# A rotary-embedding kernel: DMA runs of 64 KB instead of 32 KB, with three resident tiles

## The chip, the cores and the metric

The kernel runs on one core of a Trainium2 chip. The metric is device time in microseconds (us), the median of several executions. The profile's span, from the first to the last instruction, is some 2 us shorter than that time. Every execution has a state: slow when it took over 1.5% more than the fastest of the same kernel, else fast, and unknown for a single run. Medians are over all executions. All TensorE clocks read 1.000, in the slow executions too; the kernel does not use TensorE.

The names used below: SBUF and PSUM are the two on-chip memories in which the kernel allocates its tiles, each tile in 128 rows called partitions; VectorE and GpSimd are the engines that compute here; SyncE and ScalarE only issue DMAs. A DMA is one transfer that the program issues; it is put into the queue of the engine that issued it, and 16 DMA engines carry it out in packets. A 64 KB run is a stretch of 64 KB that is contiguous on both sides of a transfer; otherwise a run is an execution or an experiment.

## The reference

```python
def reference(x, cos, sin):          # x (16, 512, 16, 64), cos and sin (512, 32), float32
    half_dim = dim // 2              # dim = 64
    x1, x2 = x[..., :half_dim], x[..., half_dim:]
    # cos and sin broadcast over batch and heads
    first  = x1[..., :16] * cos[..., :16] - x1[..., 16:] * sin[..., :16]
    second = x1[..., :16] * sin[..., :16] + x1[..., 16:] * cos[..., :16]
    return concatenate([first, second, x2], axis=-1)
```

The input x is 33.55 MB and the output is as large. Half of every head passes through unchanged, but the kernel moves it through SBUF with the rest, because whole rows are contiguous in memory.

## The kernel before

The flat array is cut into tiles of 128 partitions; a partition holds K consecutive sequence positions, each of H x D = 1024 numbers (4 KB). With K = 8 a partition's run is 32 KB, a tile is 4 MB, and there are eight tiles.

```python
    K = 8
    T = B * S // (P * K)          # 8 tiles
    # ...
    x_pool = ctx.enter_context(tc.tile_pool(name="xp", bufs=5))
    ab_pool = ctx.enter_context(tc.tile_pool(name="abp", bufs=1))
    # ... cos and sin are loaded on the ACT queue and copied into `table`
    KC = 4
    for t in range(T):
        x_t = x_pool.tile([P, K, H, D], fp32)
        nc.sync.dma_start(out=x_t.rearrange("p k h d -> p (k h d)"), in_=xf[t])
        for k0 in range(0, K, KC):
            x1 = x_t[:, k0 : k0 + KC, :, 0:HF]
            # c and s: the table, broadcast over the heads
            nc.vector.tensor_mul(out=a_t[:], in0=x1, in1=c)
            nc.vector.tensor_mul(out=b_t[:], in0=x1, in1=s)
            nc.vector.tensor_sub(out=x1[:, :, :, 0:Q], in0=a_t[:, :, :, 0:Q], in1=b_t[:, :, :, Q:HF])
            nc.vector.tensor_add(out=x1[:, :, :, Q:HF], in0=a_t[:, :, :, Q:HF], in1=b_t[:, :, :, 0:Q])
        nc.scalar.dma_start(out=of[t], in_=x_t.rearrange("p k h d -> p (k h d)"))
```

All loads of x are issued by SyncE (queue 1), all stores and the small cos/sin loads by ScalarE (queue 10). Both queues feed the same 16 DMA engines: in the packet records never more than 16 of these packets run at once, and loads and stores take turns in the same 16 sequences. One data packet is one partition's run (1024 packets of 32 KB in each queue, for eight DMAs of 128 partitions), so a 128-partition DMA is eight packets on each engine.

## Time and profile before

| | before |
|---|---|
| time, median | 162.38 us |
| span | 160.4 us |
| bytes moved, mean rate | 67.25 MB, 419 GB/s |
| VectorE busy | 110.8 us (69%) |
| a 32 KB packet, load or store (packet records) | 1213 ns median |

From the profile page of the kernel before: the span, the busy time of the compute engines, the DMA engines' busy tenths in 40 equal slices of the span, the packets, and, for each of the two data queues, packets, MB and the time of its packets as a share of 16 engines' span.

```profile
span 160.4 us, 155 instructions
DVE 110.8 (69%) x68; POOL 0.2 (0%) x4
...
DMA  7999999999999999999999999999999999999993
...
DMA packets 2465, 67.25 MB, mean 419 GB/s; under 512 B 288, under 2 KB 416, under 8 KB 416
...
q1 hardware_dynamic: 1152, 33.55, 49.3%
q10 hardware_dynamic: 1312, 33.69, 48.7%
```

The two queue shares add to 98.0%. 98.0% of 160.4 us is 157.2 us of packets for each engine: the DMA engines are the bound, and there is next to no time without a packet. A 32 KB packet in 1213 ns is 27.0 GB/s for one engine, or 432 GB/s for 16.

The groups of VectorE work of the same page (line, engine, operation, output and inputs with shapes, count | busy us, mean ns of one | idle before it and what ended most of it):

```profile
L65 DVE TENSOR_TENSOR a_t<-x_t,table 128x2048 f32<-128x2048 f32 x16 | 36.7, 2292 | 13.6 <-DMA x_t<-in_x_dram 13.2
L66 DVE TENSOR_TENSOR b_t<-x_t,table 128x2048 f32<-128x2048 f32 x16 | 36.5, 2284 | 0.0
L67 DVE TENSOR_TENSOR x_t<-a_t,b_t 128x1024 f32<-128x1024 f32 x16 | 19.6, 1226 | 0.6
L70 DVE TENSOR_TENSOR x_t<-a_t,b_t 128x1024 f32<-128x1024 f32 x16 | 19.5, 1218 | 0.0
```

VectorE waits for data, 13.2 us in all, and has 49.6 us to spare. The same bound is seen by stage in the windows of the kernel before (stretch in us, its length, VectorE busy, GpSimd busy, clock, mean busy share of the DMA engines, GB/s):

```profile
36.00:100.00 64.00, 61.66 (x37) 0.00 (x0) 1.00 1.01 434
130.00:158.00 28.00, 12.01 (x8) 0.00 (x0) 1.00 1.00 432
```

While loads and stores run together the engines move 434 GB/s, and at the end, with stores alone, 432.

### The profile page before, as it was taken

The numbers are of one execution on the slowest core, as the hardware profiler recorded it, in microseconds if no ns is written. First come the engines' busy times: TensorE is split into PE (matmuls) and PEld (weight loads), VectorE is DVE, ScalarE is ACT, GpSimd is POOL, SyncE is SP. The second block draws the span as 40 slices with busy tenths as digits, with TensorE's granted clock in tenths as the row PEclk, the third lists the DMA queues.
The fourth block names the chain that finished last, engine by engine and source line by source line (L and its number), as shares of the span: only waits on it lengthen the run. The fifth ranks groups of instructions, "written<-read, shape, count | busy, mean of one in ns | idle before, by whom it ended". The sixth has DMA issues, their size and how long they took to land.

```text
span 160.4 us, 155 instructions
## 1 busy us (share of the span) xinstructions
DVE 110.8 (69%) x68; POOL 0.2 (0%) x4
## 2 busy tenths in 40 slices
DVE  0001599999999999999998799609995099940000
POOL 0000000000000000000000000000000000000000
DMA  7999999999999999999999999999999999999993
GB/s 253 408 400 408 392 417 490 400 408 498 400 400 474 433 392 457 457 392 449 466 392 417 490 400 408 498 400 400 476 425 400 466 441 400 449 457 400 417 482 147
DMA packets 2465, 67.25 MB, mean 419 GB/s; under 512 B 288, under 2 KB 416, under 8 KB 416
## 3 DMA queue, kind: packets, MB, share of 16 engines
q1 hardware_dynamic: 1152, 33.55, 49.3%
q10 hardware_dynamic: 1312, 33.69, 48.7%
q14 instruction: 1, 0.01, 0.0%
HBM read 33.69 MB, written 33.55 MB: 419 GB/s over the span
## 4 chain that ended last, share of the span: by engine, by line
DMA 53%; DVE 30%; issue 4%; DVEq 1%; ACTq 0%; SPq 0%
DMA x_t<-in_x_dram 21%; DMA out_dram<-x_t 21%; DVE b_t L66 11%; DMA stage<-in_sin_dram 10%; DVE a_t L65 10%; DVE x_t L70 5%; DVE x_t L67 4%; DVEq L99 1%; ACTq L41 0%; DVE table L48 0%; SPq L58 0%; DVEq L65 0%
## 5 line engine op out<-in xcount | busy, mean ns | idle before, releaser
L65 DVE TENSOR_TENSOR a_t<-x_t,table 128x2048 f32<-128x2048 f32 x16 | 36.7, 2292 | 13.6 <-DMA x_t<-in_x_dram 13.2
L66 DVE TENSOR_TENSOR b_t<-x_t,table 128x2048 f32<-128x2048 f32 x16 | 36.5, 2284 | 0.0
L67 DVE TENSOR_TENSOR x_t<-a_t,b_t 128x1024 f32<-128x1024 f32 x16 | 19.6, 1226 | 0.6
L70 DVE TENSOR_TENSOR x_t<-a_t,b_t 128x1024 f32<-128x1024 f32 x16 | 19.5, 1218 | 0.0
L48 DVE COPY table<-stage 64x256 f32<-64x256 f32 x4 | 1.1, 287 | 17.1 <-DMA stage<-in_cos_dram 12.2
L88 POOL MEMSET const-bfloat16-1.0<- 128x1 bf16 x1 | 0.1, 102 | 0.0
L88 POOL MEMSET const-uint8-127<- 128x1 uint8 x1 | 0.1, 102 | 0.0
L88 POOL MEMSET const-float32-0.0<- 128x1 f32 x1 | 0.1, 99 | 0.2 <-issue 0.2
L88 POOL MEMSET const-float32-1.0<- 128x1 f32 x1 | 0.1, 99 | 0.0
## 6 DMA issues: line engine op xcount, KB each, us to landing
x_t<-in_x_dram SPq DMA_DIRECT2D x8, 4096.0 KB, 33.9
out_dram<-x_t ACTq DMA_DIRECT2D x8, 4096.0 KB, 31.3
stage<-in_cos_dram ACTq DMA_DIRECT2D x1, 64.0 KB, 11.4
stage<-in_sin_dram ACTq DMA_DIRECT2D x1, 64.0 KB, 16.3
```

The costliest lines, as they stand in the source:

```text
L48: nc.vector.tensor_copy(out=table[r * PB : (r + 1) * PB, t], in_=stage[:, t, :, 0:Q].unsqueeze(2).to_broadcast((PB, K, 2, Q)),)
L65: nc.vector.tensor_mul(out=a_t[:], in0=x1, in1=c)
L66: nc.vector.tensor_mul(out=b_t[:], in0=x1, in1=s)
L67: nc.vector.tensor_sub(out=x1[:, :, :, 0:Q], in0=a_t[:, :, :, 0:Q], in1=b_t[:, :, :, Q:HF])
L70: nc.vector.tensor_add(out=x1[:, :, :, Q:HF], in0=a_t[:, :, :, Q:HF], in1=b_t[:, :, :, 0:Q])
L88: nc = _bacc.Bacc("TRN2", target_bir_lowering=False, num_devices=1)
L99: with _tile.TileContext(nc) as tc:
```

## The change

The intent: runs twice as long (64 KB, K = 16, four tiles of 8 MB), so fewer packets; an earlier start, because the first tile's load comes in parts of 4, 4 and 8 positions; a fine-grained end, because the last tile is loaded and stored in halves; and the scratch in PSUM with an in-place multiply, so that no scratch lies in SBUF beside the three 8 MB tiles. With three tile buffers and four tiles, the last tile's load has to wait until the first tile's store has landed.

```diff
-    K = 8
+    K = 16
...
-    x_pool = ctx.enter_context(tc.tile_pool(name="xp", bufs=5))
-    ab_pool = ctx.enter_context(tc.tile_pool(name="abp", bufs=1))
+    x_pool = ctx.enter_context(tc.tile_pool(name="xp", bufs=3))
+    b_pool = ctx.enter_context(tc.tile_pool(name="bp", bufs=2, space=bass.MemoryType.PSUM))
...                                  (table: two larger copies on VectorE, two on GpSimd)
+    loads = [[4, 4, 8]] + [[16]] * (T - 2) + [[8, 8]]
+    stores = [[16]] * (T - 1) + [[8, 8]]
...
+        for n in loads[t]:
+            nc.sync.dma_start(
+                out=x_f[:, k0 * R : (k0 + n) * R], in_=xf[t, :, k0 * R : (k0 + n) * R]
+            )
+            k0 += n
...
-            nc.vector.tensor_mul(out=a_t[:], in0=x1, in1=c)
             nc.vector.tensor_mul(out=b_t[:], in0=x1, in1=s)
+            nc.vector.tensor_mul(out=x1, in0=x1, in1=c)
...                                  (the subtraction and the addition read x1 in place of a_t)
-        nc.scalar.dma_start(out=of[t], in_=x_t.rearrange("p k h d -> p (k h d)"))
+            for lo, hi in ends:
+                if hi == k0 + KC:
+                    nc.scalar.dma_start(
+                        out=of[t, :, lo * R : hi * R], in_=x_f[:, lo * R : hi * R]
+                    )
```

More of the change, by code (lines that the diff above doesn't have):

```diff
@@ L29 @@
     REP = P // PB
+    R = H * D
     xf = x.rearrange("b s h d -> (b s h d)").rearrange("(t p f) -> t p f", t=T, p=P)
@@ L46 @@
     for r in range(REP):
-        for t in range(2):
-            nc.vector.tensor_copy(
-                out=table[r * PB : (r + 1) * PB, t],
-                in_=stage[:, t, :, 0:Q].unsqueeze(2).to_broadcast((PB, K, 2, Q)),
-            )
+        eng = nc.vector if r % 2 == 0 else nc.gpsimd
+        eng.tensor_copy(
+            out=table[r * PB : (r + 1) * PB].rearrange("p t k c j -> p (t k) c j"),
+            in_=stage.rearrange("p t k j -> p (t k) j")[:, :, 0:Q]
+            .unsqueeze(2)
+            .to_broadcast((PB, 2 * K, 2, Q)),
+        )
     C = table[:, 0].rearrange("p k c j -> p k (c j)")
@@ L55 @@
     KC = 4
+    loads = [[4, 4, 8]] + [[16]] * (T - 2) + [[8, 8]]
+    stores = [[16]] * (T - 1) + [[8, 8]]
     for t in range(T):
         x_t = x_pool.tile([P, K, H, D], fp32)
-        nc.sync.dma_start(out=x_t.rearrange("p k h d -> p (k h d)"), in_=xf[t])
+        x_f = x_t.rearrange("p k h d -> p (k h d)")
+        k0 = 0
+        for n in loads[t]:
[3 more added lines that the diff above has]
+            k0 += n
+        ends, k0 = [], 0
+        for n in stores[t]:
+            ends.append((k0, k0 + n))
+            k0 += n
         for k0 in range(0, K, KC):
@@ L62 @@
             s = Sn[:, k0 : k0 + KC].unsqueeze(2).to_broadcast((P, KC, H, HF))
-            a_t = ab_pool.tile([P, KC, H, HF], fp32)
-            b_t = ab_pool.tile([P, KC, H, HF], fp32)
-            nc.vector.tensor_mul(out=a_t[:], in0=x1, in1=c)
+            b_t = b_pool.tile([P, KC, H, HF], fp32)
             nc.vector.tensor_mul(out=b_t[:], in0=x1, in1=s)
+            nc.vector.tensor_mul(out=x1, in0=x1, in1=c)
             nc.vector.tensor_sub(
-                out=x1[:, :, :, 0:Q], in0=a_t[:, :, :, 0:Q], in1=b_t[:, :, :, Q:HF]
+                out=x1[:, :, :, 0:Q], in0=x1[:, :, :, 0:Q], in1=b_t[:, :, :, Q:HF]
             )
             nc.vector.tensor_add(
-                out=x1[:, :, :, Q:HF], in0=a_t[:, :, :, Q:HF], in1=b_t[:, :, :, 0:Q]
+                out=x1[:, :, :, Q:HF], in0=x1[:, :, :, Q:HF], in1=b_t[:, :, :, 0:Q]
             )
-        nc.scalar.dma_start(out=of[t], in_=x_t.rearrange("p k h d -> p (k h d)"))
+            for lo, hi in ends:
+                if hi == k0 + KC:
+                    nc.scalar.dma_start(
+                        out=of[t, :, lo * R : hi * R], in_=x_f[:, lo * R : hi * R]
+                    )
 _INS = ['x', 'cos', 'sin']
```

## The prediction

> **What bounds the kernel now.** The DMA engines. The page shows 67.25 MB at 419 GB/s, the two data queues busy 49.3% + 48.7%, and DMA at 9 tenths in all slices but the first and last. VectorE is busy 110.8 of 160.4 us and waits 13.2 us for loads (waits). In the packet records a 32 KB packet takes 1213 ns, a 1 KB packet 46 ns: 8 ns + bytes / 27.2 GB/s. 16 x 27.2 is 435 GB/s[...]. The 67.1 MB therefore cost 154.3 us whatever the run length; besides there are 1.7 us before the first packet, 1.2 after the last, 1 us of fixed packet cost, 1.3 us of slow packets at the start, and 1.9 us from span to time.
>
> **What the change does.**
> 1. 64 KB runs: 96 instead of 128 data packets per engine. Estimate: 32 x 8 ns = 0.3 us saved, on the bound.
> 2. Cos/sin in 32 rows of 2 KB behind 16 KB packets: the table is ready near 12 us instead of 18.3. [...] Some 0.3 us of start losses go; an earlier VectorE buys nothing by itself.
> 3. Scratch in PSUM, in-place multiply: 6.92 us per 4 rows as now (2.29, 2.28, 1.23, 1.22); not bound.
> 4. Three resident tiles of double size: the first store starts at 41 us instead of 32, and the fourth tile's load waits until that store has landed (82 us).
> 5. Last tile in halves: its end stays as fine as before.
>
> **The risk.** The queues alternate packet by packet: eight cos/sin packets needed 10 us, one between 1.21 us packets of x. So a 32 KB load of the last tile beside a 64 KB store gets a third of the rate, not half. A queue joining a busy one also starts late: the first store, issued at 32.1 us, ran its first packet at 36.0, about 2.4 packets more than the first load's 1.0 us. With 64 KB packets I estimate 6 to 7 us. Worked through packet by packet: the last half tile lands at 130 to 136 us, its 13.9 us of VectorE end at 144 to 150, and the queue has stores until 149; the DMA runs dry for up to 1 us. If the third store is issued before the second has drained, the loads get a third throughout, the last half lands near 142 and the DMA idles 6 to 8 us.
>
> **Predicted time.** 154.3 + 0.8 + 0.9 + 1.7 + 1.2 + 1.9 = 160.8 us with no gap; a small gap gives 162; the bad case 167 to 169. I say 162.2 us, range 161.0 to 168.5. Faster by over 2%: 0.02 [...]; within 2%: 0.70; slower by over 2%: 0.28.
>
> **What would show it.** 64 KB packets of 2418 ns; mean 415 to 423 GB/s; VectorE groups within 3%; VectorE idle for loads of tiles two to four. A dip of the DMA slices near 149 us, with a chain ending in the last load, two groups of VectorE operations and the last half store, shows the gap.
>
> **What would make it wrong.** 64 KB runs split into smaller packets (equal shares, no gap, 161 us); PSUM operands slowing VectorE by over 5%, which delays the last store; GpSimd copies of 5 us or more, shifting the queues into the bad case; a 64 KB pitch slower than 27 GB/s per engine.

154.3 us "whatever the run length" and the 0.3 us saved are estimates, from the packets of 1213 ns (32 KB) and 46 ns (1 KB) in the kernel before; no packet of 64 KB had been measured. The third of the rate is an estimate, too, from the turns of the cos/sin packets.

## The result, and the profile after

The changed kernel took 182.21 us (median; 180.88 to 183.55), the kernel before 162.38 us in the same rounds. A ratio in this document is the mean time of one kernel's fast runs over that of the other's fast runs of the same rounds, so it is not quite the ratio of the medians. It is 1.122 here, with a 95% interval of 1.117 to 1.127.

The page of the changed kernel, the same lines as shown of before, with the line of GB/s per slice:

```profile
span 181.8 us, 145 instructions
DVE 109.6 (60%) x66; POOL 3.1 (2%) x6
...
DMA  6999969999999999899999999999899999420595
GB/s 220 400 447 461 562 274 433 461 461 461 332 361 433 332 361 389 317 346 389 433 404 346 418 440 382 411 411 505 348 411 447 404 397 389 195 87 7 231 461 231
DMA packets 1825, 67.25 MB, mean 370 GB/s; under 512 B 224, under 2 KB 224, under 8 KB 288
...
q1 hardware_dynamic: 1008, 33.55, 46.2%
q10 hardware_dynamic: 816, 33.69, 44.5%
...
L81 DVE TENSOR_TENSOR b_t<-x_t,table 128x2048 f32<-128x2048 f32 x16 | 36.1, 2295 | 51.8 <-DMA x_t<-in_x_dram 50.8
L82 DVE TENSOR_TENSOR x_t<-x_t,table 128x2048 f32<-128x2048 f32 x16 | 36.0, 2285 | 0.1
L83 DVE TENSOR_TENSOR x_t<-x_t,b_t 128x1024 f32<-128x1024 f32 x16 | 19.4, 1214 | 0.1
L86 DVE TENSOR_TENSOR x_t<-x_t,b_t 128x1024 f32<-128x1024 f32 x16 | 19.4, 1214 | 0.0
L50 DVE COPY table<-stage 32x1024 f32<-32x1024 f32 x2 | 2.1, 1056 | 8.2 <-DMA stage<-in_sin_dram 8.2
L50 POOL COPY table<-stage 32x1024 f32<-32x1024 f32 x2 | 2.9, 1474 | 7.8 <-DMA stage<-in_sin_dram 7.8
```

VectorE is as fast as before, operation by operation (2295, 2285, 1214 and 1214 ns against 2292, 2284, 1226 and 1218); its waits for x grew from 13.2 to 50.8 us. There are two losses, and they have to be kept apart. The busy tenths show a hole near slices 35 to 38. That is one loss. The other does not show in the busy tenths: slices 11 to 20 stay at 9 tenths or near it, but the GB/s line falls from 461 to between 317 and 433. The windows of the changed kernel (columns as above) have it by stage:

```profile
20.00:38.00 18.00, 17.93 (x12) 0.00 (x0) 1.00 1.07 462
42.00:84.00 42.00, 26.75 (x16) 0.00 (x0) 1.00 0.97 364
122.00:150.00 28.00, 13.42 (x8) 0.00 (x0) 1.00 1.00 419
157.00:169.00 12.00, 12.00 (x8) 0.00 (x0) 1.00 0.13 55
```

Engines that are busy 97% of a stretch but move 364 GB/s have longer packets. The packet records say the same: 64 KB loads that run alone (before 38 us) take 2422 ns (median); over the whole run the 64 KB loads average 2689 ns (longest 4351) and the 64 KB stores 2543. (The windows with a rate above 435 have a busy share above 1.00 as well, such as 1.07 with 462 GB/s: a window counts the packets in it whole.)

The sum, from the queue shares: (46.2% + 44.5%) of 181.8 us is 164.9 us of packets for each engine, against 157.2 before, so 7.7 us are slow packets. In the packet records the engines are without a packet, between the first packet and the end of the last, for 13.9 us on average against 0.3, so 13.6 us are gaps. 7.7 + 13.6 = 21.3 us, which is the difference of the two spans (181.8 - 160.4 = 21.4).

The end of the run, from the timeline of the changed kernel (start us, duration, engine, line, operation, [idle before <- what ended it]):

```profile
156.28 4.50 DVE L81 TENSOR_TENSOR b_t<-x_t,table 128x2048 f32<-128x2048 f32 x2 [19.69 <-DMA x_t<-in_x_dram]
...
168.49 1.21 DVE L86 TENSOR_TENSOR x_t<-x_t,b_t 128x1024 f32<-128x1024 f32 x1
169.73 0.34 ACTq L91 DMA_DIRECT2D out_dram<-x_t  x1
```

The last half tile lands at 156.3 us. VectorE then works 13.4 us, and only at 169.7 us can the last store be issued. By then the other stores have drained, so the engines stand nearly empty (55 GB/s between 157 and 169 us). The page's chain of waits (the work that ended last, followed back) is no help for this stretch: it puts 48% of the span down to "another core or an unknown queue". The timeline shows it.

Issue times of the changed kernel, from the trace: first store 38.5 us, second store 71.8, the last tile's two loads 91.7 and 92.0 (after the first store had landed), third store 118.3, the last two stores 136.6 and 169.7.

### The profile page after: what moved, and what is told of

The parts are those of the page before. It is cut to its first block, busy times and chain, and to the rows that moved or that the text cites. A ratio compares the mean times of both kernels' runs of the same rounds, so it can differ in the third digit from the quotient of the medians.

```text
span 181.8 us, 145 instructions
## 1 busy us (share of the span) xinstructions
DVE 109.6 (60%) x66; POOL 3.1 (2%) x6
## 3 DMA queue, kind: packets, MB, share of 16 engines
q1 hardware_dynamic: 1008, 33.55, 46.2%
q10 hardware_dynamic: 816, 33.69, 44.5%
## 4 chain that ended last, share of the span: by engine, by line
another core or an unknown queue 48%; DMA 29%; DVE 13%; issue 1%; DVEq 1%; SPq 0%
DMA x_t<-in_x_dram 29%; DVE x_t L82 5%; DVE b_t L81 4%; DVE x_t L83 2%; DVE x_t L86 2%; DVEq L119 1%; SPq L68 0%; DVEq L81 0%
## 5 line engine op out<-in xcount | busy, mean ns | idle before, releaser
L81 DVE TENSOR_TENSOR b_t<-x_t,table 128x2048 f32<-128x2048 f32 x16 | 36.1, 2295 | 51.8 <-DMA x_t<-in_x_dram 50.8
L82 DVE TENSOR_TENSOR x_t<-x_t,table 128x2048 f32<-128x2048 f32 x16 | 36.0, 2285 | 0.1
L83 DVE TENSOR_TENSOR x_t<-x_t,b_t 128x1024 f32<-128x1024 f32 x16 | 19.4, 1214 | 0.1
L86 DVE TENSOR_TENSOR x_t<-x_t,b_t 128x1024 f32<-128x1024 f32 x16 | 19.4, 1214 | 0.0
L50 DVE COPY table<-stage 32x1024 f32<-32x1024 f32 x2 | 2.1, 1056 | 8.2 <-DMA stage<-in_sin_dram 8.2
L50 POOL COPY table<-stage 32x1024 f32<-32x1024 f32 x2 | 2.9, 1474 | 7.8 <-DMA stage<-in_sin_dram 7.8
```

What stands on the lines that cost most here:

```text
L50: eng.tensor_copy(out=table[r * PB : (r + 1) * PB].rearrange("p t k c j -> p (t k) c j"), in_=stage.rearrange("p t k j -> p (t k) j")[:, : ...
L82: nc.vector.tensor_mul(out=x1, in0=x1, in1=c)
L83: nc.vector.tensor_sub(out=x1[:, :, :, 0:Q], in0=x1[:, :, :, 0:Q], in1=b_t[:, :, :, Q:HF])
L86: nc.vector.tensor_add(out=x1[:, :, :, Q:HF], in0=x1[:, :, :, Q:HF], in1=b_t[:, :, :, 0:Q])
```

## The experiments

Each experiment starts from the changed kernel unless it says otherwise. "Slow ratio" is a packet's recorded time over the time of an undisturbed packet of its size (2418 ns for 64 KB, 1213 ns for 32 KB; a bare figure such as 1.2 beside packets is this ratio). Where the text speaks of the packets of one engine, the sequence was put together from the records, by joining each packet to the one that began when it ended; the trace does not name the engine.

### Packet lengths: e1, e2, e3, e5

The first question was which direction's packet length matters. All three of the following keep the tiles and buffers of the changed kernel.

e1, every 64 KB DMA cut into two of 32 KB runs:

```diff
-    loads = [[4, 4, 8]] + [[16]] * (T - 2) + [[8, 8]]
+    loads = [[4, 4, 8]] + [[8, 8]] * (T - 1)
...
-                    nc.scalar.dma_start(out=of[t, :, lo * R : hi * R], in_=x_f[:, lo * R : hi * R])
+                    for m in range(lo, hi, 8):
+                        nc.scalar.dma_start(
+                            out=of[t, :, m * R : (m + 8) * R], in_=x_f[:, m * R : (m + 8) * R])
```

> Changed kernel with every 64 KB run cut into two DMAs of 32 KB runs, loads and stores, both stores of a tile still issued together when the tile is done. Tiles of 16 rows, three resident, 64 KB row pitch, PSUM scratch and table copies stay. Theory A (the length of the packets is the cause: 64 KB packets run slower when loads and stores are mixed, and share the rate unequally): packets back to 1213 ns in both directions while mixed, last half load lands by 130 us, no dry stretch, 161 to 163 us. Rival B (the 64 KB pitch of the addresses slows the mixed traffic): packets stay over 1.05 times 1213 ns while mixed, 170 us or more. Rival C (three resident tiles give the schedule too little slack whatever the packets): packets at 1213 ns, yet a dry stretch before the last store, 167 us or more.

Measured: 162.78 us, ratio 1.003 (1.001 to 1.005). Packets of 1213 ns (medians) in both directions, idle 0.3 us. The tiles, the buffers, the PSUM scratch and the GpSimd copies together cost nothing. The loss went with the 64 KB runs, but the moment at which the store joins changed as well: its first half was issued at 25.2 us instead of 38.5.

e2, only the loads cut:

> Changed kernel with 32 KB runs for all loads, 64 KB runs kept for the stores of the first three tiles. If any 64 KB packet in mixed traffic is slow, the 64 KB stores stay near 1.05 to 1.1 times 2418 ns and the time lies between, 164 to 175 us. If only 64 KB loads are slow (they were 1.25 times in the changed kernel, the stores 1.08), packets are at full rate and the time is 161 to 164 us. If unequal shares alone make the trouble, loads get a third here all the time and the last half load lands at 127 us or later; by alternation worked out packet by packet this alone still ends without a dry stretch.

Measured: 174.70 us, ratio 1.076 (1.073 to 1.080). The first store was issued at 38.55 us. From 43 us on the packets were slow on 11 of the 16 engines (their first dozen averaged 1.09 to 1.21), while four of the other five averaged 1.01 to 1.02 and one 1.13. So the loads need not be of 64 KB.

e3, only the stores cut:

> Changed kernel with 64 KB runs kept for the loads of the second and third tile, all stores with 32 KB runs. If 64 KB loads are the slow ones, they stay at 1.2 times 2418 ns while mixed and the time is 164 to 175 us; if slowness needs 64 KB on both sides or comes from the stores, packets are at full rate and the time is 161 to 163 us. Unequal shares now favour the loads and cannot delay the last tile.

Measured: 162.31 us, ratio 0.999 (0.998 to 1.001). The 64 KB loads took 2418 ns (median; mean 2434). So the loss is gone without 64 KB stores. But cutting the store has the side effect seen in e1: its first half depends on half the tile only, and was issued at 25.3 us instead of 38.5. This run alone does not say which of the two helped.

e5, the same with the two halves issued in reverse order, which was meant to keep the first store back until the tile is done:

> As the run with stores in 32 KB runs, but both 32 KB stores of a tile are issued only when the whole tile is done (second half first), as the 64 KB store of the changed kernel is. It takes the earlier start of the first store (25 us instead of 38) out of that run. If the length of the store packets is the cause: 64 KB loads at 2418 ns while mixed, 161.5 to 163 us. If the earlier, finer stores were what helped: slow packets and 170 us or more.

Measured: 162.33 us, ratio 1.000 (0.998 to 1.002), but the scheduler still issued a store at 25.2 us. The run repeats e3 and does not test the delay.

### The same issue times with 32 KB packets: e6

A 256-byte gap in the middle of each partition's run in SBUF leaves the same DMAs at the same points of the program, but in packets of 32 KB:

```diff
-        x_t = x_pool.tile([P, K, H, D], fp32)
+        x_t = x_pool.tile([P, 2, 8 * R + 64], fp32)
...                                  (loads, stores and the rotation skip the gap)
```

> The changed kernel with the same DMAs, each issued at the same point and moving the same rows, but with a gap of 256 bytes in the middle of each partition's tile, so that the 8 MB DMAs are made of 32 KB packets. Nothing but packet length changes. If packet length is the cause: packets of 1213 ns while mixed, last half load lands by 132 us, 161 to 165 us. If the size of the DMAs or the three resident tiles are the cause: 170 us or more.

Measured: 164.29 us, ratio 1.012 (1.009 to 1.016), first store issued at 38.65 us. On every engine one load packet, the last before the first store packet, was slow (1.22 to 1.53). The same is seen in runs without the loss (e1: up to 1.64, e9: up to 1.41), so it is not the loss. The next 30 packets of every engine, loads and stores in turn, ran at 1.00. Some packets were slow again between 86 and 99 us and between 113 and 117 us (up to 1.98), and then no more. This run holds more than it seems to: on all 16 engines its packets stood in the order that is found slow further down (e12, e13: each store packet directly behind the load packet of the same number). At 32 KB this order ran at full rate.

### The unequal share: e7 and e4

e7 cuts only the first tile's store into 32 KB runs, and leaves the second and third at 64 KB:

> The changed kernel with only the first tile's store in 32 KB packets (both halves issued when the whole tile is done); second and third store stay 64 KB. It separates the two parts of the theory: the slow packets of 42 to 84 us should be gone, so the last tile's loads are issued near 83 us instead of 92. If the unequal share (32 KB loads beside 64 KB stores) then makes the late last half by itself: it lands at 138 to 147 us, a dry stretch follows, 166 to 173 us. If the slow packets were the whole cause: 161 to 164 us.

Measured: 171.94 us median; ratio 1.050 (1.045 to 1.055). The profile is of a run that counts as slow (173.06 us), so it is used for the order of events only. The two halves were not held back until the whole tile was done, as the expectation had it: as in e5 a store was issued early, at 25.3 us. So the run does not show that the length of the first store's packets removes the slowness. After a few loads of up to 1.17 as the store joined (27 us), there were no slow packets until 105 us, the last tile's loads were issued at 81.6 us, and yet its last half landed at 145.8 us and the engines ran nearly dry. The window of e7:

```profile
152.00:159.00 7.00, 7.00 (x6) 0.00 (x0) 1.00 0.04 19
```

This is the unequal share that the prediction described, by itself. The packet records show the turns: one 32 KB load, one 64 KB store, and so on. The changed kernel has 131 such turns; with a load of 1213 ns and a store of 2418 ns a turn took 3.62 us from one load to the next (median of all 3.70). So the loads of an engine get 32 KB in 3.62 us, 9.0 GB/s, a third of the 27.0 above, as long as a 64 KB store is queued.

e4 loads the last tile in one DMA of 64 KB runs, so that load and store packets are equally long, as in the kernel before, where the two directions got 218 and 215 GB/s (packet records, 40 to 100 us):

> Changed kernel with the last tile loaded in one DMA of 64 KB runs instead of two halves; stores as in the changed kernel. If the unequal share of the last tile's 32 KB loads beside 64 KB stores makes the late last half (156 us) and the dry stretch, the whole tile should now land near 130 to 140 us, with VectorE's 27 us behind it: 166 to 175 us. If the slow packets are the cause, the last load still lands at 145 us or later and the time is 185 us or more.

Measured: 176.18 us, ratio 1.085 (1.083 to 1.087). The windows of e4:

```profile
42.00:84.00 42.00, 26.75 (x16) 0.00 (x0) 1.00 0.98 384
100.00:130.00 30.00, 15.83 (x11) 0.00 (x0) 1.00 1.00 433
```

In this run the same kinds of packets, 64 KB loads beside 64 KB stores, were slow in one stretch and at full rate in a later one. Length alone is therefore not the cause of slowness. The time lies between the two cases of the expectation, just above the first. The whole tile landed at 135.0 us, within the 130 to 140 expected, but VectorE then had the whole tile's 26.6 us to do, the last store was issued at 161.7 us, and the engines were idle 8.7 us. So loading the tile whole moves the gap and does not close it.

### Is VectorE's traffic the cause? e8, e9, e10

e8 takes all VectorE work out (a copy, wrong); e9 replaces it with work of about the same length inside PSUM (wrong); e10 is the copy with 90 VectorE additions in SBUF beside it (wrong).

```diff
-            nc.vector.tensor_mul(out=b_t[:], in0=x1, in1=s)
-            ...
+            e = x_t[:, k0, 0, 0:1]                                   # e9
+            nc.vector.tensor_scalar_mul(out=z_t[:], in0=z_t[:], scalar1=e)
+            nc.vector.tensor_scalar_mul(out=z_t[:], in0=z_t[:], scalar1=0.5)
+            nc.vector.tensor_scalar_mul(out=z_t[:, 0:1600], in0=z_t[:, 0:1600], scalar1=0.5)
+            nc.vector.tensor_add(out=e, in0=e, in1=z_t[:, 0:1])      # z_t lies in PSUM
```

> The changed kernel without the rotation (output wrong on purpose: x is copied): the same loads and stores, no VectorE work between them. Measures whether 64 KB loads beside 64 KB stores are slow by themselves. If so: both queues' 64 KB packets average over 1.05 times 2418 ns in the mixed part. If VectorE's traffic in SBUF has a part in it: 2418 ns.

Measured: 162.22 us (one run, state unknown). 64 KB stores and loads 2418 ns (medians), with both directions running. The first store was issued at 23.3 us.

> The changed kernel's loads and stores with VectorE work of about the same length per 4 rows, but reading and writing PSUM only (output wrong on purpose: x is copied; one element per 4 rows is touched to keep the waits). The first store is issued near 38 us, as in the changed kernel. If the slow packets come from how the two queues' 64 KB packets meet when the store joins late: slow packets (over 1.05 times 2418 ns) from 42 us on, late last half, 175 us or more. If they come from VectorE's traffic in SBUF: packets at 2418 ns, the last half decided by the unequal share alone, 161 to 171 us.

Measured: 162.55 us, ratio 1.001 (0.998 to 1.004). Packets at full rate, idle 0.4 us.

> The copy without rotation, with 90 VectorE additions of 1024 elements (two SBUF inputs, SBUF output) on a tile of their own running from 11 us to some 120 us, which no DMA waits for (output wrong on purpose). If VectorE's SBUF traffic slows 64 KB packets: over 1.05 times 2418 ns in 30 to 100 us, 168 us or more. If it has no part: as the copy alone, 162 us.

Measured: 166.45 us, ratio 1.025 (1.022 to 1.028). Fifteen engines ran at 1.00; one, out of step with the rest, had slow packets (1.23 to 1.43). The time fits neither case of the expectation, and why this one engine was slow is not shown.

e9 looked like proof that VectorE's SBUF traffic slows the packets. It was not: its first store was issued at 37.2 us instead of 38.5, and the next runs show that this is what counted.

### Moving the moment at which the store joins: e11 to e14

One, two or three VectorE multiplications of 1.2 us ahead of the first rotation delay everything that follows; e12 does it to e9.

```diff
+    d_t = const_pool.tile([P, 1024], fp32)
+    tf = table.rearrange("p t k c j -> p (t k c j)")
+    for _ in range(1):                       # e13: 2, e14: 3
+        nc.vector.tensor_mul(out=d_t[:], in0=tf, in1=tf)
```

The theory that e11 was to test: on some engines the first store packet comes before, on others after, a given load packet ("straddle"), and this disorder makes them slow.

> The changed kernel, correct output, with one VectorE multiplication of 1.2 us added before the first tile, so that the first store is issued near 39.8 us instead of 38.5, half a 64 KB packet later. Theory S (straddle): in the changed kernel the store's packets reach the 16 engines just as these choose their next packet, some take it at once, the others one packet later; from then on some engines store while others load, and that state is the slow one. Then half a packet of delay lets all engines take it at the same turn: packets at 2418 ns between 42 and 80 us, the first store lands near 80 to 83 us, 161 to 172 us in all (with or without the gap of the unequal share). If VectorE's SBUF traffic beside 64 KB packets is the cause, nothing changes: 180 us or more.

Measured: 183.28 us, ratio 1.127 (1.121 to 1.133). All 16 engines started the first store packet within 44.3 to 44.7 us, so they were in step, and slow. The theory of the straddle falls, at least as the only way to slow packets.

> The run with VectorE work in PSUM alone (which had packets at 2418 ns, first store issued at 37.2 us), with the same 1.2 us added, so that its first store is issued near 38.5 us, where the changed kernel issues it. Theory S: it now straddles, some engines load while others store, packets over 1.05 times 2418 ns between 42 and 80 us, 168 us or more, with no SBUF traffic of VectorE. If VectorE's SBUF traffic is the cause: 162 to 163 us as before.

Measured: 183.06 us, ratio 1.124 (1.118 to 1.130). Here is the window from 42 to 84 us, first of e9, then of e12:

```profile
42.00:84.00 42.00, 26.58 (x16) 0.00 (x0) 1.00 1.04 449
```

```profile
42.00:84.00 42.00, 26.58 (x16) 0.00 (x0) 1.00 0.99 365
```

The two kernels differ in one multiplication of 1.2 us, which also has to wait for the table; the first store was issued at 39.4 instead of 37.2 us. VectorE's work within the window is the same to the last digit, and it is in PSUM (but for one element per 4 rows). The rate falls from 449 to 365 GB/s and the time rises by 20.5 us. VectorE's SBUF traffic is not needed for the loss.

What differs is the order of packets on each engine. In e9 the first store's packets 0 and 1 followed the last packet of the second tile's load, and only then came packet 0 of the third tile's load. In e12 the first store's packet 0 directly followed packet 0 of the third tile's load, and so on with packets 1, 2 and 3.

> The changed kernel with two such multiplications, so that the first store is issued near 41 us, one whole 64 KB packet later than in the changed kernel. Theory S predicts that it straddles again: slow packets, 175 us or more. If the delay itself was the remedy, it is as fast as the run with one.

Measured: 180.16 us median; ratio 1.101 (1.097 to 1.104). This run holds both cases at once. Two engines' sequences of e13, L for a 64 KB load and S for a 64 KB store, start in us / slow ratio:

```
typical of 14 engines:  L#0 42.0/1.00  L#1 44.5/1.12  S#0 47.2/1.00  L 49.6/1.00  S 52.0/1.00  L 54.4/1.00
one of 2 engines:       L#0 42.2/1.00  S#0 44.6/1.43  L 48.1/1.10    S 50.8/1.31  L 53.9/1.00  S 56.3/1.32
```

On 14 engines two packets of the third tile's load went ahead of the first store packet; their next ten packets averaged 1.00 to 1.02. On two engines one load packet went ahead; their next ten averaged 1.22 and 1.23, with single packets up to 1.56 later. At the same time, in the same program, it is the order on the engine that goes with the rate. The two slow engines ended their last packet of the first store at 86.7 and 86.9 us, the others at 80.7 to 81.2 us, and the last tile's loads, which wait for that store, were issued at 87.6 us.

e4 had such a split too: five engines in the order of e9 averaged 1.00 to 1.01 over ten packets (their loads slowed to 1.2 to 1.3 from 66 us on), eleven in the order of e12 averaged 1.09 to 1.19. Counted over the profiles in which the first store joins the third tile's load with 64 KB packets both ways (the changed kernel, e4, e9, e11 to e15): on 74 of 74 engines in the order of e12 the first ten packets averaged 1.08 or more, and on 51 of 54 engines in another order at most 1.02.

> The changed kernel, correct output, with three of the 1.2 us multiplications, first store issued near 42.2 us. Theory P (same partition): an engine's 64 KB packets are slow when [...] the first store's packet number 0 directly follows packet number 0 of the third tile's load (started at 41.8 us); engines whose store comes one load packet later are not slow (in the run with two multiplications 14 engines came late and ran at 2418 ns, 2 came early and were slow). At 42.2 us all 16 should come one packet later: 64 KB packets within 1.02 of 2418 ns on average between 50 and 80 us, first store landed by 85 us. Time 161 to 172 us, with or without the gap of the unequal share. Rival (a late join is slow in itself, or the state is chance): over 1.05, first store landed after 88 us.

Measured: 172.42 us, ratio 1.064 (1.060 to 1.069), with the first store issued at 42.3 us. All 16 engines now had two load packets ahead of the first store packet (46.7 to 47.2 us). The packets did what the expectation said of them; the time is at the edge of its 161 to 172 us. The page and the windows of e14:

```profile
span 169.6 us, 148 instructions
...
q1 hardware_dynamic: 1008, 33.55, 46.6%
q10 hardware_dynamic: 816, 33.69, 46.0%
```

```profile
47.00:84.00 37.00, 27.51 (x18) 0.00 (x0) 1.00 1.01 436
152.00:162.00 10.00, 5.49 (x5) 0.00 (x0) 1.00 0.37 157
```

Delaying the program by 3.7 us made it 10 us faster than the changed kernel. The packets run at full rate: 92.6% of 169.6 us is 157.0 us, as before the change. The last tile's loads were issued at 81.5 us, ten microseconds earlier than in the changed kernel. What remains is the unequal share alone: the third store was issued at 105.9 us, while the second one was still in the queue, so nearly every engine alternated 32 KB load and 64 KB store to the end. The last half landed at 144.1 us, the last store was issued at 157.5 us, and the engines were idle 9.4 us.

### Memory addresses or SBUF partitions? e15 to e18

Each of the eight packets that an engine has of a 128-partition DMA is one partition's run. The guess, the same-partition theory of e14 to e18: in the slow order a load packet stands directly before the store packet of the same partition, at the same place of its tile in memory, and in the fast orders the two belong to different partitions. The records name no partition, so no run shows whether this is so; the clause that took it as known is cut from the expectation of e14. In e6 the numbers of neighbouring packets agree in the same way, and its 32 KB packets were not slow, so a conflict of this kind would have to depend on the packets' length.

e15 shifts the output by 53 rows of 4 KB (212 KB) in memory, so that the two packets no longer stand at the same place of their tiles. The last tile's store wraps round in small pieces; this lengthens the tail, so only 42 to 90 us is read.

```diff
+    OFF = 3 * N + 5 * R                      # N = 16 * R, R = 4 KB
...
+                    nc.scalar.dma_start(out=rows_at(t * P * N + OFF, P), in_=x_f[:, :])
```

> The changed kernel with the output written 212 KB further on in DRAM (wrapping round at the end; output wrong on purpose), all else up to the last tile as it is: same moment of the first store, same SBUF partitions, but no store goes to the address in its tensor that a load of the same partition number reads in its own. If the slow packets come from the pair of DRAM addresses: 2418 ns between 45 and 80 us. If from the pair of SBUF partitions, or from anything else that the shift leaves alone: over 1.1 times 2418 ns as in the changed kernel, first store landed near 91 us.

Measured: 205.0 us, ratio 1.260 (1.253 to 1.268), tail included. The profile is of a run that counts as slow (207.21 us). The window of e15:

```profile
42.00:84.00 42.00, 26.75 (x16) 0.00 (x0) 1.00 0.96 360
```

360 GB/s against 364 in the changed kernel, and the last tile's load issued at 91.1 us against 91.7. Fifteen engines were in the slow order. The sixteenth was in the order of e9 and slow all the same (1.22 over ten packets). The slowness does not need the two packets at the same place of their tiles in memory. This does not exclude every relation of addresses, since only one shift was tried.

e16 and e17 were to change the pairing without moving the moment: each store is two DMAs of 64 partitions, the upper half first in e16, the lower half first in e17. e18 is e16 with the last tile loaded whole.

```diff
-                    nc.scalar.dma_start(out=of[t, :, lo * R : hi * R], in_=x_f[:, lo * R : hi * R])
+                    for p0 in (64, 0):                                # e17: (0, 64)
+                        nc.scalar.dma_start(
+                            out=of[t, p0 : p0 + 64, lo * R : hi * R],
+                            in_=x_f[p0 : p0 + 64, lo * R : hi * R])
```

> Every store is two DMAs of 64 partitions, partitions 64 to 127 first; the same bytes in the same packet lengths, issued at the same points (first store at 38.5 us, its first packets at 42 to 44.6 us). The same-partition theory (a load packet and the store packet beside it on an engine run slow when both are of one SBUF partition, and so of the rows at one place of their tiles): if the packets go round the engines row by row, a store packet now stands four packets away from the load packet of its own partition, so the 64 KB packets between 45 and 80 us take 2418 to 2440 ns, the first store lands at 82 to 84 us, and what is left is the unequal share at the last tile: 170 to 174 us, ratio near 1.06, as in the runs that had that fault alone. The rival, that the slowness comes from where the join falls in time (any store joining at 38 to 40 us): slow packets as before, first store landing near 91 us, 180 to 184 us.

> The control of the run with partitions 64 to 127 first: the same two DMAs for each store, partitions 0 to 63 first. The same-partition theory, if packets go round the engines row by row: nothing changes in the order of the packets against the changed kernel, slow packets from 42 us on, first store landing at 90 to 92 us, 179 to 185 us. If instead each engine has a block of neighbouring rows, half a store of 64 rows pairs other rows too, and this run is as fast as the other, near 172. The rival, that more and smaller DMAs are what helps: as fast as the other run.

> Both faults taken away at 64 KB: stores with partitions 64 to 127 first, and the last tile loaded by one DMA of 64 KB packets, so that it shares equally with the stores. Same-partition theory and the theory of the unequal share together: first store lands at 82 to 84 us, the last load is issued there and lands at 105 to 125 us, no dry stretch, 161 to 163 us, ratio 0.99 to 1.005. If slow packets come anyway when the second or third store joins: 165 to 176 us (the kernel with the last load whole and stores in one DMA took 176.2).

Measured: e16 214.05 us, ratio 1.319 (1.313 to 1.326); e17 214.63 us, ratio 1.321 (1.319 to 1.324); e18 213.66 us median, ratio 1.307 (1.302 to 1.312). All three expectations failed, for a reason that has nothing to do with the pairing. The window of e16 in which the stores of the last tile run with no load beside them:

```profile
192.00:212.00 20.00, 0.00 (x0) 0.00 (x0) 1.00 0.97 211
```

A store of 64 partitions gets 211 GB/s, half of the 432 of the stores of 128 partitions in the kernel before (130 to 158 us), with the engines busy 97% of the window. Between 94 and 103 us, too, 64 KB store packets alone took 5108 ns, 2.1 times 2418. Why they take twice as long is not shown. The three runs say nothing about the pairing.

## Why the prediction was wrong

Clean cases from the experiments (e9 and e14) let the sum be taken apart. Packet time per engine is the recorded time of all data packets over 16; idle is the time from the first packet to the end of the last, less that.

| run | packet time per engine, us | idle, us | time, us |
|---|---|---|---|
| before | 157.2 | 0.3 | 162.38 |
| e9: full rate, no gap | 157.2 | 0.4 | 162.55 |
| e1: all 32 KB | 157.6 | 0.3 | 162.78 |
| e14: full rate, unequal share | 157.1 | 9.4 | 172.42 |
| changed kernel: slow packets, unequal share | 164.9 | 13.9 | 182.21 |

**"64 KB packets of 2418 ns".** This step failed. The prediction took 8 ns + bytes / 27.2 GB/s from the loads and stores of the kernel before, where it held while both directions ran. It held at 64 KB when loads ran alone, and in e8, e9 and e14 with both directions. In the changed kernel it did not: loads averaged 2689 and stores 2543 ns, and the stretch from 42 to 84 us ran at 364 GB/s. Directly this is 7.7 us. The prediction listed "a 64 KB pitch slower than 27 GB/s per engine" among what would make it wrong, but gave it no size and left it out of the range; and it is not the pitch, since the same pitch ran at 449 GB/s in e9.

**What decides whether packets are slow.** Shown: VectorE's SBUF traffic is not needed (e12), and engines out of step are not needed (e11); the 64 KB length is not enough by itself (e8, e9, e14), and the order is not enough by itself (e6, at 32 KB). In these runs it took both: stores of 64 KB runs (with loads of 64 KB, or of 32 KB as in e2), and an order in which the store packet directly follows the load packet with the same number within its DMA (74 of 74 engines slow, against 3 of 54 in other orders). The three exceptions, two engines of the changed kernel (1.06 and 1.08, with single loads up to 1.5) and one of e15 (1.22), each ran beside engines in the slow order; they are not explained. The reason below the order, such as a conflict inside one SBUF partition, is not shown: the runs that were to separate it from the moment of joining failed for another reason, and one shift of the output (e15) is the only evidence against memory addresses.

**"The last half tile lands at 130 to 136 us".** Measured: 156.3 us. The prediction had the course of events (packet-by-packet turns, a third of the rate, when the bad case comes) and mis-sized it twice. First, slow packets moved the landing of the first store from the 82 us that it expected to 91.7, and the last tile's loads wait for that; e14, without slow packets, issued them at 81.5. Second, it gave the bad case a low weight. e14 is the bad case with nothing else wrong: the last half landed at 144.1 us where 142 was predicted, the idle time was 9.4 us where 6 to 8 were, and the kernel took 172.4 us where 167 to 169 were. e7 fell into the same case by another way. e9, whose first store was issued at 37.2 us, escaped it: its second store had drained before the third came in, and the loads between 108 and 115 us ran alone. e9 and e14 issued the first store 5.1 us apart (37.2 and 42.3 us) and fell into different cases; the prediction took the good one as the likely one, and even its bad case, at 167 to 169 us, was some 4 us short of e14.

**The dry stretch "up to 1 us", "6 to 8 us" in the bad case.** Measured: 13.6 us more idle than before, of which the unequal share by itself accounts for about 9 (e14: 9.4 - 0.3 = 9.1). The other 4.5 us, the rest of the difference, go together with the slow packets, which pushed the last loads further back.

**What was right.** DMA is the bound, and "faster" did not come: 64 KB packets save about 0.3 us by the estimate (32 packets of 8 ns less), and no run got clearly below the kernel before (the best, e3, is at 0.999 with an interval that includes 1). VectorE groups were within 3% (2295, 2285, 1214, 1214 ns against 2292, 2284, 1226, 1218), so neither the PSUM operand nor the in-place multiply cost anything. The table was ready and the first rotation began at 11.2 us (about 12 predicted). The first store was issued at 38.5 us, somewhat earlier than the 41 predicted; its first packets started 3.6 to 6.1 us later (42.1 to 44.6 us), against 3.9 us in the kernel before (32.1 to 36.0) and the 6 to 7 us estimated. The end has the predicted form: last load, two groups of VectorE operations, last half store.

A version that beats both kernels was not found. e1 and e3 have the new tiling and neither fault, and are level with the kernel before, as the bound lets one expect.

## What to carry to other kernels

Here the profile showed DMA engines busy in every slice and 434 GB/s, the rate of undisturbed packets (432 GB/s from 1213 ns for 32 KB). Longer runs then had only the fixed cost of a packet to win (an estimated 0.3 us), while they made the packet-by-packet turns coarser (a 32 KB load every 3.62 us beside 64 KB stores); check first how a short packet on the critical path will share with the long ones of the other queue. Read busy share and GB/s together: in the changed kernel the engines that were 97% busy at 364 GB/s had slow packets, and at 13% they were waiting for an issue, and these two losses need different cures. When a variant is unexpectedly fast, shift it by a microsecond or two with harmless work before believing the reason: here a delay of 2.2 us in the first store's issue turned 162.6 us into 183.1.
